# A hybrid encoder step: nine projections as Strassen groups behind the recurrence, with a slot table for all engines

## The chip, the cores and the metric

The kernel runs on one core of a Trainium2 chip. The metric is the device time of one execution in microseconds, lower is better; profiled executions give a span from the first to the last instruction.

## What is computed

One layer of a streaming encoder over 2112 tokens: 2048 of a new stream (16 tiles of 128) and 64 of a running one (the sample, tile 17). From the reference:

```python
xn = rms_norm(x, norm_gain)
u = xn @ w_in                                   # 1024 -> 8 x 1024 columns
xa, za, q, k, v, zb, ga, gb = split_in(u)
xc = conv_b + sum(xpad[:, j:j + T] * conv_w[j] for j in range(CONV_W))
h, h_last = rglru(xc, h0, is_first, ...)        # gates from two block-diagonal products, then a scan
ya = h * jax.nn.silu(za)
q = rms_norm(q.reshape(B, T, H_B, 2, DK), q_norm_gain)
k = rms_norm(k.reshape(B, T, H_B, 2, DK), k_norm_gain)
o = diff_attn(q, k, v, ...)                     # 8 heads, chunk-causal; the sample sees 4096 cached keys
yb = (rms_norm(o, subln_gain) * (1.0 - lam_init)) * jax.nn.silu(zb)
m = jax.nn.sigmoid(ga) * (ya @ w_proj_a) + jax.nn.sigmoid(gb) * (yb @ w_proj_b)
y = x + m @ w_out
```

All of it is float32. Outputs are y, the keys, the values, the last convolution rows and the last recurrence state.

## The kernel before

Every projection is a float32 product made of three passes of the rounded type float32r: an operand is cut into a high part (a rounded copy) and a low part (a subtraction), and `mm3` (L68 to L71) multiplies high by high, high by low and low by high into the same PSUM bank. TensorE runs in the order in which the program issues its work (`manual_schedule`); the other engines are ordered by the compiler's scheduler. The kernel has four stages.

The first (L120 to L347) loads x tile by tile, normalizes it (`norm_x`), transposes it (`turn_x`) and keeps the high and low parts of all of normalized x, channels on partitions, in SBUF (`xh`, `xl`) until the end of the second stage. Values, queries and keys come in twelve blocks of 256 columns: for each token tile `mm_tok` makes 24 matmuls of 256 columns into `acca`, with x as the stationary operand. Queries and keys are normalized per head (`norm_qk`: square, reduction, root, Newton step, scaling) and transposed (`turn_qk`).

The second (L349 to L496) runs over eight channel blocks n. For each, `mm_grp` makes five products (convolution input xa, its gate za, zb, ga, gb) of 128 channels with x as the moving operand, in five token groups of 512, 512, 384, 384 and 320 columns, 24 matmuls per group, into five rotating banks `accb`. `hawk` does the convolution, `gates` the two small gate products one matmul group later, `scan_half` the recurrence of half the tokens; their tiles R, IX, SZ and A have one buffer each. `gated` writes the three gates to DRAM, channel-major.

The third is attention (L498 to L1022), interleaved by a model written in the kernel. Where a head ends, `finish` scales the outputs, and `part` transposes them, multiplies them by the gate zb out of PSUM and writes yb.

The fourth (L1024 to L1086) does the three output projections with weights stationary and activations moving, six groups of 352 tokens, 24 matmuls each per 128 output columns; `load_w3` and `load_g` cut weights and activations on ScalarE, VectorE and GpSimd, and the result is written transposed. Loads and stores go through SP's queue, but for a few on GpSimd's.

The lines around which the change turns are these:

```python
for t in range(0, NT, 2):                       # first stage, per block of 256 columns
    mm_tok(acc[:, j, :], t + j, ws)
for n in range(KT):                             # second stage
    wxa, wza = load_w1(5 * n), load_w1(5 * n + 1)
    hawk(n, wxa, wza)
    gated(load_w1(5 * n + 2), zb_d, n, True)
    gated(load_w1(5 * n + 3), ga_d, n, False)
    gated(load_w1(5 * n + 4), gb_d, n, False)
```

## Time and profile before

| what | value |
|---|---|
| median of 3 runs | 3072.23 us (3063.8 to 3074.84) |
| the profiled execution's span | 3068.5 us |
| first stage (values, queries, keys) | 0 to 663 us |
| second stage (recurrence and gates) | 663 to 1631 us |
| third stage (attention) | 1631 to 2494 us |
| change of stage | 2494 to 2506 us |
| fourth stage (projections) | 2506 to 3065 us |

PE is TensorE's matmuls, PEld its weight loads, DVE VectorE, ACT ScalarE, POOL GpSimd, SPq the queue that issues DMAs. `L57` is line 57 of the kernel, and `out<-in` names the tile that is written and those that are read. In groups the number after the comma is the mean length of one instruction in ns, and what stands after the second bar is the engine's idle time before it. Matmuls are pipelined, so their durations overlap; the distance of their starts is what one costs.

### The profile page before, as it was taken

What the parts mean: (1) busy time and instruction counts of PE and PEld (TensorE: products, weight loads), DVE (VectorE), ACT (ScalarE), POOL (GpSimd) and SP (SyncE); (2) the same over time, 40 slices, a digit from 0 to 9 for tenths busy, and PEclk for the clock granted to TensorE, in tenths of its full rate; (3) what the DMA queues carried; (4) which work ended last, traced back from release to release, by engine and by line L of the source; (5) the groups of instructions that cost most, each with busy time, mean ns of one, the idle gap of its engine ahead of it and who ended that gap; (6) DMA issues with size and microseconds to landing.
All of it is one profiled execution on the core that took longest, in us unless ns stands there. A gap on an engine that the chain in (4) does not pass through costs nothing.

```text
span 3068.5 us, 50185 instructions
## 1 busy us (share of the span) xinstructions
PE 2982.8 (97%) x19448; PEld 2787.9 (91%) x19448; DVE 1322.6 (43%) x3439; ACT 1135.1 (37%) x2179; POOL 1065.5 (35%) x1011
## 2 busy tenths in 40 slices
PE   7999999999999999999998999999999989999999
PEld 7999999999999998999896888888888889999999
DVE  7015454413314224133135667767776761232311
ACT  5112222213224223223134766676676651110100
POOL 1113233222212222122114666666666652222220
PEclk9999999999999999999999999999999999999999
DMA  5223333322121121121117344444543343433322
GB/s 173 81 83 115 125 124 129 120 83 72 39 75 58 43 83 50 45 77 42 64 47 212 107 143 128 127 138 135 147 115 123 94 155 110 122 118 90 94 94 91
DMA packets 208350, 312.37 MB, mean 102 GB/s; under 512 B 33760, under 2 KB 132944, under 8 KB 208112
## 3 DMA queue, kind: packets, MB, share of 16 engines
...
q14 instruction: 84, 0.69, 0.1%
...
## 4 chain that ended last, share of the span: by engine, by line
PE 84%; DVE 7%; ACT 3%; issue 2%; DMA 2%; POOL 1%; SPq 0%; POOLq 0%; ACTq 0%; DVEq 0%
PE accb L71 8%; PE accb L70 8%; PE accb L69 8%; PE acca L69 6%; PE acca L70 6%; PE acca L71 6%; PE acc L71 6%; PE acc L69 6%; PE acc L70 6%; PE accv L640 6%; PE pk L574 3%; PE pk L575 3%; PE ptt L632 3%; PE accv L763 2%; PE pk L695 1%
## 5 line engine op out<-in xcount | busy, mean ns | idle before, releaser
L71 PE MATMUL accb<-xh,wl 128*128 128x512 f32 (+2 forms) x1600 | 562.5, 352 | 0.0
L69 PE MATMUL accb<-xh,wh 128*128 128x512 f32 (+2 forms) x1600 | 562.3, 351 | 0.0
L70 PE MATMUL accb<-xl,wh 128*128 128x512 f32 (+2 forms) x1600 | 562.2, 351 | 0.0
L69 PE MATMUL acca<-wh,xh 128*128 128x256 f32 (+1 forms) x1632 | 469.1, 287 | 0.0
L70 PE MATMUL acca<-wl,xh 128*128 128x256 f32 (+1 forms) x1632 | 461.7, 283 | 2.1 <-DVE wl L131 1.6
L71 PE MATMUL acca<-wh,xl 128*128 128x256 f32 (+1 forms) x1632 | 461.3, 283 | 0.0
L71 PE MATMUL acc<-gh,wl 128*128 128x352 f32 x1152 | 373.6, 324 | 0.0
L69 PE MATMUL acc<-gh,wh 128*128 128x352 f32 x1152 | 373.1, 324 | 0.0
L70 PE MATMUL acc<-gl,wh 128*128 128x352 f32 x1152 | 370.8, 322 | 0.0
L69 PEld LDWEIGHTS accb<-xh,wh 128*128 128x128 f32 x1600 | 300.4, 188 | 25.6
L70 PEld LDWEIGHTS accb<-xl,wh 128*128 128x128 f32 x1600 | 300.3, 188 | 25.5
L71 PEld LDWEIGHTS accb<-xh,wl 128*128 128x128 f32 x1600 | 300.3, 188 | 25.3
L69 PEld LDWEIGHTS acca<-wh,xh 128*128 128x128 f32 (+1 forms) x1632 | 307.7, 189 | 5.4 <-ACT vst L341 3.8
L70 PEld LDWEIGHTS acca<-wl,xh 128*128 128x128 f32 (+1 forms) x1632 | 307.8, 189 | 2.8 <-DVE wl L131 1.8
L71 PEld LDWEIGHTS acca<-wh,xl 128*128 128x128 f32 (+1 forms) x1632 | 307.5, 188 | 0.0
L640 PE MATMUL accv<-v,tw 128*128 128x128 f32 x2176 | 295.3, 278 | 6.3 <-ACT o L652 6.2
L574 PE MATMUL pk<-k,Q 128*128 128x512 f32 (+2 forms) x640 | 266.3, 417 | 29.6 <-DVE mp L595 19.9
L56 POOL TENSOR_SCALAR wh<-raw 128x512 fp32r<-128x512 f32 x125 | 81.7, 654 | 607.9 <-PE accb L70 364.6
L587 DVE TENSOR_SCALAR_CACHE_REDUCE S<-pk,far 128x1024 f32<-128x1024 f32 x224 | 225.8, 1014 | 141.4 <-PE pk L575 131.5
L640 PEld LDWEIGHTS accv<-v,tw 128*128 128x128 f32 x2176 | 270.7, 194 | 10.9 <-ACT o L652 8.3
L605 ACT ACTIVATE S<-S,nm 128x1920 f32<-128x1920 f32 (+7 forms) x128 | 209.0, 1633 | 74.8 <-DVE nm L604 73.3
L575 PE MATMUL pk<-k,Q 128*128 128x512 f32 (+2 forms) x640 | 232.8, 369 | 1.0 <-DMA Q<-ql_d 1.0
...
## 6 DMA issues: line engine op xcount, KB each, us to landing
...
```

Source lines behind the costliest of these rows:

```text
L56: nc.gpsimd.tensor_scalar(hi, src, 1.0, 1.0, op0=ALU.mult, op1=ALU.mult)
L69: nc.tensor.matmul(out, shi, mhi, start=start, stop=False)
L70: nc.tensor.matmul(out, shi, mlo, start=False, stop=False)
L71: nc.tensor.matmul(out, slo, mhi, start=False, stop=stop)
L574: nc.tensor.matmul(pk[:, o], Q[0][:, m, qs], kk, start=True, stop=False)
L575: nc.tensor.matmul(pk[:, o], Q[1][:, m, qs], kk, start=False, stop=True)
L587: nc.vector.tensor_scalar(s[:, k0 : k0 + f], pk[:, :f], far[:, h : h + 1], None, op0=ALU.add, op1=ALU.max, accum_out=mp[:, cx["j"] : cx["j ...
L605: nc.scalar.activation(s[:, :n], s[:, :n], AF.Exp, bias=nm, accum_out=sc[m])
L632: nc.tensor.transpose(ptt[:, j, :], ss[r][:, kt * P : (kt + 1) * P], ident)
L640: nc.tensor.matmul(acc[:, r, :], tw[:, j, :], hd[kt // 8][1][:, kt % 8, :], start=kt == r == 0, stop=kt == 2 * p + 1)
L695: nc.tensor.matmul(pk[:, us], Q, kc[:, us], start=True, stop=True)
L763: nc.tensor.matmul(acc, tw[:, j, :], vc[:, (j8 % 2) * 4 + j, :], start=j8 == 0 and j == 0, stop=False)
```

## The change

The recurrence comes first and alone: per channel block only xa and za are multiplied, with three banks instead of five (three more are for the transposes of x, which now happen inside the first block). Normalized x is put together again on GpSimd (`keep_x`, inside blocks two to four) and written to DRAM.

The nine other projections (values; queries and keys of four heads, twice; zb; ga; gb; the two branch projections; the output projection) become nine groups of 1024 columns. A group takes token tiles in pairs (i and i + 8), cuts x, weights and result into quarters and makes seven products of quarters instead of eight (Strassen's scheme in Winograd's form), each 12 matmuls of 512 columns, with x stationary. The sums of x quarters are made for each pair (`plan_x`), those of weights for each group (`plan_w`), on VectorE and GpSimd. The sample tile has its own form, five slots of 8 matmuls. Time is counted in slots, one for each product: every step of every engine is entered for a slot, and `tick` issues the steps of a slot behind its product, so that TensorE, VectorE, ScalarE and GpSimd all run in the order of the program. Activations and gates are now token-major in DRAM, the gate zb multiplies attention's output before the transpose, and between the second and the third projection the merged activations are transposed on TensorE.

```diff
+class Stage:
+    def __init__(self, nc, tc, c, name, ident):
+        self.nc, self.ident = nc, ident
+        kw = dict(reuse_waits=RW)
+        E = mybir.EngineType
+        c.enter_context(tc.manual_schedule(engines={E.PE, E.DVE, E.Activation, E.Pool}))
+        self.xo = c.enter_context(tc.tile_pool(name="xo" + name, bufs=20, **kw))
+        self.wq = c.enter_context(tc.tile_pool(name="wq" + name, bufs=17, **kw))
+        self.sb = c.enter_context(tc.tile_pool(name="sb" + name, bufs=14, **kw))
+        self.wk = c.enter_context(tc.tile_pool(name="wk" + name, bufs=3, **kw))
+        self.pm = c.enter_context(tc.tile_pool(name="pm" + name, bufs=5, space=PSUM, **kw))
+        self.pt = c.enter_context(tc.tile_pool(name="pt" + name, bufs=3, space=PSUM, **kw))
+        self.now = -99
+        self.tasks = {}
+
+    def at(self, s, fn):
...
+    def plan_w(self, src, ws, b):
+        nc, q, at = self.nc, {}, self.at
+
+        def load(nm, i):
+            q[nm] = self.wtile()
+            for k in range(0, 4, 2):
+                nc.sync.dma_start(q[nm][:, k : k + 2, :], src[i, :, k : k + 2, :])
+
+        def sub(dst, x, y, over=None):
+            q[dst] = q[over] if over else self.wtile()
+            for i in range(2):
+                s = slice(2 * i, 2 * i + 2)
+                nc.vector.tensor_tensor(q[dst][:, s, :], q[x][:, s, :], q[y][:, s, :], op=ALU.subtract)
+
+        def cut(nm):
+            raw = q[nm]
+            hi, lo = self.wtile(F32R), self.wtile(F32R)
+            for i in range(2):
+                s = slice(2 * i, 2 * i + 2)
+                nc.scalar.copy(hi[:, s, :], raw[:, s, :])
+                eng = nc.vector if i == 0 else nc.gpsimd
+                eng.tensor_tensor(lo[:, s, :], raw[:, s, :], hi.bitcast(F32)[:, s, :], op=ALU.subtract)
+            ws[nm] = hi, lo
+
+        at(b - 16, lambda: (load("B11", 0), load("B12", 1)))
+        at(b - 13, lambda: sub("T1", "B12", "B11"))
+        at(b - 10, lambda: load("B22", 3))
+        at(b - 9, lambda: (load("B21", 2), cut("B11")))
+        at(b - 7, lambda: sub("T2", "B22", "T1"))
+        at(b - 6, lambda: cut("T2"))
+        at(b - 5, lambda: sub("T3", "B22", "B12", "B12"))
+        at(b - 4, lambda: sub("T4", "B21", "T2", "T2"))
+        for i, nm in enumerate(("T3", "T1", "B21", "T4", "B22")):
+            at(b - 3 + i, lambda nm=nm: cut(nm))
+
...
+        u, v = item, item + 8
+        at(b - 9, lambda: (load("A21", v, 0), load("A22", v, 1)))
+        at(b - 8, lambda: (load("A11", u, 0), load("A12", u, 1)))
+        at(b - 6, lambda: add(V, "S1", "A21", "A22", ALU.add))
+        at(b - 5, lambda: (add(V, "S2", "S1", "A11", ALU.subtract), add(G, "S3", "A11", "A21", ALU.subtract, "A21")))
+        at(b - 4, lambda: hi("A11"))
+        at(b - 3, lambda: (lo("A11", G), hi("S2")))
+        at(b - 2, lambda: (lo("S2", V), add(G, "S4", "A12", "S2", ALU.subtract), hi("S3")))
+        at(b - 1, lambda: (lo("S3", G), hi("S1")))
+        at(b, lambda: (lo("S1", G), hi("A12")))
+        at(b + 1, lambda: (lo("A12", V), hi("A22"), lo("A22", G)))
+        at(b + 2, lambda: hi("S4"))
+        at(b + 3, lambda: lo("S4", G))
+
+    def product(self, out, a, b, start, stop, more=False):
+        for kt in range(4):
+            mm3(self.nc, out, a[0][:, kt, :], a[1][:, kt, :], b[0][:, kt, :], b[1][:, kt, :],
+                start and kt == 0, stop and kt == 3, more)
+
+    def pair(self, item, x, w, done):
+        nc = self.nc
+        bank = lambda: self.pm.tile([P, 512], F32, name="acc")
+        V = nc.vector
+        b1 = bank()
+        self.product(b1, x["A11"], w["B11"], True, True)
+        u2 = self.small()
+        nc.scalar.copy(u2, b1)
+        self.tick()
+        b2 = bank()
+        self.product(b2, x["S2"], w["T2"], True, True)
+        V.tensor_tensor(u2, u2, b2, op=ALU.add)
+        self.tick()
+        b3 = bank()
+        self.product(b3, x["S3"], w["T3"], True, True)
+        c22 = self.small()
+        V.tensor_tensor(c22, u2, b3, op=ALU.add)
+        self.tick()
+        b4 = bank()
+        self.product(b4, x["S1"], w["T1"], True, True)
+        V.tensor_tensor(c22, c22, b4, op=ALU.add)
+        done(item + 8, 1, c22)
+        self.tick()
+        self.product(b1, x["A12"], w["B21"], False, True, True)
+        c11 = self.small()
+        nc.scalar.copy(c11, b1)
+        done(item, 0, c11)
+        self.tick()
+        self.product(b3, x["A22"], w["T4"], False, True, True)
+        c21 = self.small()
+        V.tensor_tensor(c21, u2, b3, op=ALU.add)
+        done(item + 8, 0, c21)
+        self.tick()
+        self.product(b4, x["S4"], w["B22"], False, True, True)
+        V.tensor_tensor(u2, u2, b4, op=ALU.add)
+        done(item, 1, u2)
+        self.tick()
...
+        bank = lambda: self.pm.tile([P, 512], F32, name="acc")
+        b2 = bank()
+        product(b2, x["A0"], w["B11"], True, False)
+        self.tick()
+        b1 = bank()
+        product(b1, x["A0"], w["B11"], True, False)
+        self.tick()
+        product(b2, x["A0"], w["T1"], False, False)
+        self.tick()
+        product(b1, x["A1"], w["B21"], False, True)
+        out(0, b1)
+        self.tick()
+        product(b2, x["A1"], w["B22"], False, True)
+        out(1, b2)
+        self.tick()
+
+
+    def run(self, groups):
+        plan, b = [], 0
+        for g, (wsrc, xsrc, out) in enumerate(groups):
+            ws = {}
+            self.plan_w(wsrc, ws, b)
+            for it in ITEMS:
+                xs = {}
+                self.plan_x(xsrc, it, xs, b)
+                plan.append((it, xs, ws, out, b))
+                b += 5 if it == "s" else 7
+        self.now = -20
+        while self.now < 0:
+            self.tick() if self.now in self.tasks else self.skip()
+        for it, xs, ws, out, b in plan:
+            assert self.now == b
+            done = out(it, b)
+            if it == "s":
+                self.sample(xs, ws, done)
+            else:
+                self.pair(it, xs, ws, done)
+        while self.tasks:
+            self.tick() if self.now in self.tasks else self.skip()
+
+    def skip(self):
...
+        pm = c1.enter_context(tc.tile_pool(name="pmb", bufs=3, space=PSUM))
+        pg = c1.enter_context(tc.tile_pool(name="pgb", bufs=2, space=PSUM))
...
+        def keep_x(t, half):
+            g, o, tn = tokslice(t)
+            ks = slice(half * 4, half * 4 + 4)
+            raw = wr.tile([P, 4, P], F32, name="raw")
+            nc.gpsimd.tensor_tensor(
+                raw[:, :, :tn], xh[g].bitcast(F32)[:, ks, o : o + tn], xl[g].bitcast(F32)[:, ks, o : o + tn], op=ALU.add
+            )
+            nc.sync.dma_start(xn_d[t, :, ks, :tn], raw[:, :, :tn])
...
+        for n in range(1, KT):
+            hawk(n, load_w1(2 * n), load_w1(2 * n + 1), next_keep)
+        while pend:
+            _, fn, args = pend.pop(0)
+            fn(*args)
...
+        S.run([
+            (I["wg"][0], xn_d, out_v),
+            (I["wg"][1], xn_d, out_qk(0)),
+            (I["wg"][3], xn_d, out_gate(zb_d, True)),
+            (I["wg"][2], xn_d, out_qk(4)),
+            (I["wg"][4], xn_d, out_gate(ga_d, False)),
+            (I["wg"][5], xn_d, out_gate(gb_d, False)),
+        ])
...
+            def weigh(b, nb):
+                tn = TOK[b][1]
+                zt = wk.tile([P, 4, P], F32, name="zt")
+                nc.sync.dma_start(
+                    zt[:tn, :nb, :], zb_d[b : b + nb, :tn, h * P : (h + 1) * P].rearrange("b p c -> p b c")
+                )
+                nc.vector.tensor_tensor(o[:tn, b : b + nb, :], o[:tn, b : b + nb, :], zt[:tn, :nb, :], op=ALU.mult)
...
+                nc.scalar.mul(yt[:, :nb, :tn], pb[:, :nb, :tn], gs)
...
+                at(S.now + 1, lambda: nc.gpsimd.tensor_tensor(c[:tn], c[:tn], gt.pop((t, half))[:tn], op=ALU.mult))
+                at(S.now + 2, lambda: nc.vector.tensor_tensor(c[:tn], c[:tn], mt.pop((t, half))[:tn], op=ALU.add))
...
+        S.run([
+            (I["wg"][6], ya_d, out_a),
+            (I["wg"][7], yb_d, out_b),
+            (I["wg"][8], mt_d, out_y),
+        ])
```

## Rows read from the trace of the kernel before

**Rows 1.** Page, busy time of the span: engine, us, share, instructions.

```profile
PE 2982.8 (97%) x19448; PEld 2787.9 (91%) x19448; DVE 1322.6 (43%) x3439; ACT 1135.1 (37%) x2179; POOL 1065.5 (35%) x1011
```

**Rows 2.** Busy time by stretch: stretch, length, each engine, granted clock, DMA share, GB/s.

```profile
0.00:12.14 12.14, 0.00 (x0) 0.03 (x1) 2.40 (x10) 2.98 (x6) 1.41 (x7) 1.00 0.69 240
12.14:80.00 67.86, 61.23 (x484) 59.27 (x485) 56.70 (x132) 41.98 (x91) 9.85 (x10) 0.97 0.48 156
...
12.14:663.00 650.86, 644.23 (x5319) 634.98 (x5320) 273.69 (x740) 169.67 (x416) 171.26 (x241) 1.00 0.31 112
663.00:1630.70 967.70, 961.84 (x5042) 876.71 (x5042) 291.37 (x475) 287.85 (x405) 241.59 (x270) 1.00 0.19 62
905.00:1026.00 121.00, 120.36 (x633) 109.77 (x632) 36.44 (x59) 35.71 (x50) 30.36 (x33) 1.00 0.17 59
1630.70:2494.00 863.30, 815.73 (x5624) 715.80 (x5622) 612.59 (x1981) 595.71 (x1254) 520.75 (x412) 0.98 0.44 129
2494.00:2506.00 12.00, 1.77 (x12) 1.50 (x13) 10.31 (x19) 5.23 (x10) 8.03 (x9) 0.64 0.76 237
2506.00:3065.00 559.00, 559.00 (x3457) 558.93 (x3456) 131.76 (x214) 73.63 (x91) 122.47 (x74) 1.00 0.36 110
```

**Rows 3.** Timeline of TensorE, first and last matmul of steady runs: start, us, operation.

```profile
20.77 1.03 PE L186 MATMUL ptx<-ident,big 128*128 128x128 f32 x8
...
561.09 0.28 PE L71 MATMUL acca<-wh,xl 128*128 128x256 f32 x1
...
564.09 0.28 PE L69 MATMUL acca<-wh,xh 128*128 128x256 f32 x1
...
722.23 0.40 PE L69 MATMUL accb<-xh,wh 128*128 128x512 f32 x1
...
727.70 0.33 PE L69 MATMUL accb<-xh,wh 128*128 128x384 f32 x1
```

**Rows 4.** Groups by line and shape: busy us, mean ns; L1042 by line: minimum, median, maximum ns.

```profile
L447 DVE TENSOR_TENSOR IX<-sz,xc 128x512 f32<-128x512 f32 x2 | 1.4, 688 | 2.7 <-ACT sz L446 2.7
...
L1042 DVE TENSOR_TENSOR wl<-raw,wh x24: 1214/1225/2735, 2496.7 to 2872.9; 128x1024 fp32r<-128x1024 f32 x24
...
L207 DVE TENSOR_REDUCE va<-sqa 128x8 f32<-128x512 f32 x62 | 42.5, 686 | 254.7 <-ACT sqa L205 254.7
...
L64 DVE SCALAR_TENSOR_TENSOR ya<-tmpa,ya 128x8 f32<-128x8 f32 x61 | 34.4, 564 | 2.1
L246 DVE SCALAR_TENSOR_TENSOR big<-ptx,gq,big 128x256 fp32r<-128x256 f32 x61 | 29.0, 475 | 0.0
...
L57 POOL TENSOR_TENSOR wl<-raw,wh 128x512 fp32r<-128x512 f32 x125 | 162.3, 1299 | 9.7
...
L1058 POOL TENSOR_TENSOR gl<-rg,gh 128x704 fp32r<-128x704 f32 x48 | 83.1, 1741 | 239.1 <-ACT gh L1057 238.8
```

**Rows 5.** VectorE beside GpSimd: two timelines, and two lines with minimum, median, maximum ns.

```profile
L428 DVE SCALAR_TENSOR_TENSOR xc<-xa,chan,xc x120: 544/749/1519, 672.0 to 1562.0; 128x512 f32<-128x512 f32 x48, 128x384 f32<-128x384 f32 x48, 128x324 f32<-128x324 f32 x24
...
712.11 1.52 DVE L428 SCALAR_TENSOR_TENSOR xc<-xa,chan,xc 128x324 f32<-128x324 f32 x1
...
711.97 1.30 POOL L57 TENSOR_TENSOR wl<-raw,wh 128x512 fp32r<-128x512 f32 x1
...
2499.19 1.66 POOL L1058 TENSOR_TENSOR gl<-rg,gh 128x704 fp32r<-128x704 f32 x1 [2.97 <-ACT gh L1057]
2499.20 1.67 DVE L62 SCALAR_TENSOR_TENSOR e<-yo 128x2 f32<-128x2 f32 x1
...
L1077 DVE TENSOR_TENSOR M<-acc,gt x48: 510/525/529, 2515.2 to 2694.1; 128x352 f32<-128x352 f32 x48
```

**Rows 6.** Timelines of ScalarE and VectorE, from one half of a recurrence block to the next.

```profile
691.86 0.48 ACT L402 COPY xa<-accb 128x384 f32<-128x384 f32 x1 [3.59 <-PE accb L71]
...
708.17 1.21 DVE L477 TENSOR_TENSOR SZ<-SZ,R 128x1024 f32<-128x1024 f32 x1
...
713.55 1.00 DVE L417 TENSOR_TENSOR SZ<-sz,accb 128x384 f32<-128x384 f32 x2
```

946 lines of the change are left out of this document (511 added, 435 removed).

## The prediction

> **What bounds the kernel now.** Read the busy table first: TensorE is busy 97% of the span [rows 1]. That word is cheap, since a waiting pipeline can look busy, so the stretches come next [rows 2]. In the value/query/key stretch, in the gate/recurrence stretch and in the projection stretch at the end TensorE has no gap worth naming, while VectorE, ScalarE and GpSimd are busy for a fifth to two fifths. Only attention (815.7 of 863.3 us) and the 12 us between attention and the projections show TensorE idle. Last comes the distance between the starts of matmuls, which is what one really costs (the durations in rows overlap): 24 of 512 columns take 5.47 us, 0.228 each; 25 of 256 columns take 3.00 us, 0.120 each [rows 3]. So each projection stretch costs its matmul count times that distance, and two things can make it shorter: fewer matmuls, or wider ones. The profiled execution spans 3068.5 us; the median of the runs is 3072.2. I add 3.7 us to a sum made in this execution.
>
> **The change, part by part. 1. Products.** Nine products of 1024 columns leave their old forms. Before: 4896 matmuls of 256 columns (values, queries, keys) x 0.120 = 587.5 us. Gates: one pass of the channel loop takes 121.0 us [rows 2] for five column blocks and 30 small recurrence products (12,696 columns at 0.228 per 512 = 5.7 us), so a block is 23.06 us and the 24 gate blocks 553.5 us. Output projections: the whole stretch, 559.0 us. Together 1700 us. After: seven half-size products instead of eight, each 4 slices x 3 passes = 12 matmuls of 512 columns. A pair of token tiles is 84 x 0.228 = 19.14 us; a group is 8 pairs plus 40 matmuls for the sample tile (9.12 us) = 162.3 us; nine groups 1460 us. New on TensorE are 136 transposes of the merged activations, 0.109 us each ((1.03 - 0.27)/7 in [rows 3]) = 14.8 us. The other transposes are as many as before. Saved on TensorE: 225 us. This is the sure part, because the same matmul form (128x128 stationary, 512 moving) stands in the trace.
>
> **2. The recurrence first.** Per channel block TensorE now has 2 x 23.06 + 5.7 = 51.8 us; VectorE keeps 36.4 us less five gate multiplications (some 2.9 us) = 33.5 us, so it fits. Not so the first block, which now also carries the normalization of x. There VectorE did 59.1 us for 17 tiles up to 80 us [rows 2]: 3.4 us per tile without the weights, some 3.65 with the split multiplication: 62 us. With constants (5), fast weights (1.4) and the 20 of 33.5 us that lie ahead of the last column group, started at 8 us (by 12.14 it had done 2.4), this makes 96 us; the last two products add 7: 103 us, where TensorE alone would need 79. Blocks two and three also write the normalized x out again: 15 GpSimd additions each (1.30 us [rows 4]). I take 55 us each (bounds 52, all hidden, and 63, the sum of GpSimd's 38 us and VectorE's 25 us with two SBUF inputs, one after the other), 53 for the fourth and 52 for the rest. Stage: 103 + 110 + 53 + 208 = 474 us (450 to 520).
>
> **3. Who feeds TensorE in the groups.** This is the dangerous part. Before, weights and activations were split once and stayed; now every pair needs 4 VectorE and 7 GpSimd operations of 128x512 to make its sums and low parts, and every group needs 15 VectorE and 7 GpSimd halves of 128x1024 for its weights. Prices [rows 4]: VectorE 0.69 (512) and 1.23 (1024); GpSimd 1.30 (512) and, by the step from 512 to 704 (0.44 us), 2.48 (1024). GpSimd in a plain group: 8 x 9.1 + 17.4 = 90 of 162 us. In the first two projection groups four products of gate and result per pair are added (5.2 us): 134 of 162 and of 177. VectorE in the two query/key groups, per pair: 17 operations of 0.69 (4 for x, 5 out of PSUM, 4 reductions, 4 scalings) = 11.7, two low parts of queries 1.5, two chains of root and Newton steps 2.7: 15.9; weights 18.4/8 = 2.3: 18.2 us against 19.14 + 1.7 = 20.9 us on TensorE.
>
> These two engines don't run free of each other. The trace shows it three times [rows 5]: a VectorE operation of 128x324 with two SBUF inputs that takes 0.54 alone takes 1.52 when it starts inside a GpSimd subtract, and ends 0.36 after it; a Newton step of two columns takes 1.67 beside a subtract of 1.66; the product that reads PSUM never took over 0.53. The wait is a little shorter than the whole: 1.16 + 0.54 would be 1.70, measured 1.52. So an operation with two SBUF inputs waits out the other engine's, about half a GpSimd operation each time. In a query/key pair 14 VectorE operations are of that kind and GpSimd is busy two thirds: 14 x 2/3 x 0.6 = 5.6 us; 18.2 + 5.6 = 23.8 against 20.9, 2.9 us per pair, 24 per group, with the weight boundary 28 (0 to 45). The Trainium skill, in "SBUF — State Buffer", section "Who interferes with whom", states this as an exclusive lock: a VectorE instruction with two SBUF inputs and a GpSimd instruction that reads SBUF block each other for a whole instruction. By that rule taken whole the groups would go as in rival B below; the trace agrees with the lock, short of the 0.18 us just worked out.
>
> Where groups meet, the weights' 35.8 us of VectorE and GpSimd work fall into 13 slots before the group and 6 slots of it (8 x 2.73 + 5 x 1.82 + 6 x 2.73 = 47 us), beside 24 us of x work (6 left of the last pair, 1 for the sample, 17 for the next two pairs): 59 us with whole durations, less where they overlap. I take 4 us where the neighbours are light (twice), 6 after the gate group with SiLU, 28 with each query/key group, 10 at each of the two boundaries of the projections: 90 us in all (0 to 180).
>
> **4. Seams.** Recurrence to groups: the weight space is the old x space and comes free only as the last block uses it; 12 us (2 to 25). Groups to attention: 5 (0 to 12), the first keys wait for x tiles. Attention: weighting by the gate moves ahead of the transpose, VectorE's product stays one, ScalarE gets 41 copies in 863 us; I take 863 (-5 to +10), since the transposes there waited only a little on VectorE. Attention to projections: 12 us now, with DMA at 237 GB/s [rows 2]; the first group needs 4 MB of weights and 1 MB of x, 21 us at that rate, some of it ahead: 22 (12 to 35). Queue: all of these loads sit on SP, and a store that waits for a result holds the loads behind it; the table issues loads 8 to 16 slots ahead (22 us and more), which covers a landing of 3 to 5 us. End: a DMA and two additions more: 8 instead of 3.5.
>
> Sum: 474 + 12 + (6 x 162.3 + 272 x 0.109 + 2 = 1005) + 70 + 5 + 863 + 22 + (3 x 162.3 + 14.8 = 501.6) + 20 + 8 = 2980; plus 3.7: **2984 us**, 88 less than the median.
>
> **Rivals. A, TensorE stays fed.** The slot leads of 3 to 5 slots (8 to 14 us) swallow the waits: no 90, the first seam 4, the second 0, the third 12, the recurrence 450: 2847 us. For it: GpSimd has 90 of 162 us in five groups. Against: query/key and the two projection groups.
> **B, the shared path sets the pace.** GpSimd and two-input VectorE work add up with whole durations: first projection group 132 + 41 = 173 against 162 us (+11), second, with 4 more additions on VectorE per pair, 197 against 177 (+20), 12 us at each of seven boundaries (84), query/key 30 each: 175 instead of 90 us, 3069 us (3040 to 3095). For it: [rows 5]. Against: the 0.18 us of overlap per wait, over some 100 waits in a group. The page named above, taken whole, would give this.
> **C, slower: a convoy.** All four engines run in emission order. If in the four crowded groups each of the 61 slots waits for one more GpSimd subtract, 244 x 1.30 = 317 us come in place of 76: 3225 us. It takes the whole gain from 0.67 us per slot ((88 + 76)/244). Against: results are two slots old when their bank is written again.
> **D, three banks.** The recurrence has 3 PSUM banks for its products where it had 5, and one buffer for the gated product: from the evacuation at 691.86 to the end of the product that frees it 17.5 us pass, and the bank of the next half goes free after 713.55 [rows 6]. If TensorE waits there, 5.5 and 4 us per block, 65 in all: 3048 us. Against: with two banks held the third still turns over.
>
> **How the numbers follow.** Chances: forecast 0.54 (2900 to 3040), A 0.15, B 0.15, D 0.06, C 0.10. The range reaches down to the upper half of A and up to B's middle: 2855 to 3070; outside are half of A, some of B, and C. This kernel's measurement can tell about 0.5% from no change, so faster is below 3057 and slower above 3087. Faster: 0.53 + 0.15 + 0.06 + 0.04 = 0.78; within: 0.01 + 0.07 + 0.02 = 0.10; slower: 0.10 + 0.02 = 0.12.
>
> **What would show it.** Right: groups of about 162 us in plain stretches, query/key groups near 205, x work on VectorE lengthened from 0.69 towards 1.5 while GpSimd subtracts, TensorE's idle time ending on VectorE or GpSimd operations of the weights near group starts, the recurrence over at about 474 us. Wrong: TensorE idle in every slot (C), idle ended by the gated product's buffer (D), a pair above 19.5 us without any wait (the matmul price), or attention longer by more than 10 us.

## The result and the profile after

The changed kernel takes 3253.1 us in the median, the kernel before 3073.1 us in the same series: a ratio of 1.059 (95% interval 1.058 to 1.061). The forecast was 2984 us with a range of 2855 to 3070. Both the sign and the range were missed. The profiled execution spans 3249.5 us.

The busy table of after, to set beside [rows 1] (engine, us, share, instructions):

```profile
PE 2866.6 (88%) x14808; PEld 2396.7 (74%) x14808; DVE 2111.9 (65%) x3884; ACT 1564.5 (48%) x2871; POOL 1826.5 (56%) x1311
```

TensorE has fewer instructions, as meant, but it is busy 88% of the span instead of 97%; VectorE and GpSimd have risen from 43% and 35% to 65% and 56%.

Busy time by stretch in after, the counterpart of [rows 2] (stretch, length, PE, PEld, DVE, ACT, POOL, granted clock, DMA share, GB/s):

```profile
0.00:127.00 127.00, 81.52 (x448) 72.64 (x449) 91.70 (x252) 83.01 (x166) 23.63 (x32) 0.87 0.30 101
127.00:526.00 399.00, 375.15 (x1898) 335.86 (x1896) 261.63 (x382) 187.25 (x240) 182.71 (x165) 0.97 0.19 61
526.00:559.00 33.00, 0.27 (x2) 0.01 (x1) 16.49 (x16) 11.62 (x12) 2.80 (x2) 0.55 0.49 176
559.00:1709.00 1150.00, 1050.59 (x4560) 840.89 (x4560) 760.39 (x900) 484.49 (x850) 662.09 (x423) 0.96 0.42 132
1709.00:1729.00 20.00, 0.03 (x1) 0.06 (x1) 1.50 (x3) 2.70 (x4) 7.02 (x18) 0.54 1.02 263
1729.00:2656.00 927.00, 837.35 (x5632) 727.02 (x5632) 620.87 (x1998) 613.34 (x1296) 531.25 (x410) 0.96 0.42 118
2656.00:2675.00 19.00, 0.17 (x1) 0.00 (x0) 8.95 (x7) 4.91 (x7) 2.47 (x2) 0.50 0.94 336
2675.00:3241.00 566.00, 521.34 (x2272) 420.26 (x2272) 347.76 (x325) 176.62 (x299) 414.52 (x262) 0.95 0.49 164
3241.00:3249.50 8.50, 0.16 (x1) 0.00 (x0) 2.57 (x4) 0.58 (x1) 0.00 (x0) 0.63 0.26 63
```

The reader can lay this beside the forecast's sum, stretch by stretch (boundaries by first and last matmul):

| stretch | forecast, us | measured, us | missed by |
|---|---|---|---|
| recurrence | 474 | 526 | +52 |
| to the groups | 12 | 33 | +21 |
| six groups | 1075 | 1150 | +75 |
| to attention | 5 | 20 | +15 |
| attention | 863 | 927 | +64 |
| to the projections | 22 | 19 | -3 |
| three groups | 522 | 566 | +44 |
| end | 8 | 8 | 0 |

The misses add up to 268 us, and no single one explains the result. That is why the experiments go stage by stage.

What was right is seen in a plain pair (first line; 86 matmuls and no idle time) beside a query/key pair (second line):

```profile
1050.00:1069.00 19.00, 19.00 (x86) 15.74 (x85) 9.66 (x13) 7.07 (x15) 10.13 (x8) 1.00 0.31 111
822.80:845.60 22.80, 21.14 (x102) 17.20 (x101) 18.95 (x31) 10.87 (x21) 12.01 (x9) 1.00 0.54 162
```

The plain pair takes 19.0 us, forecast 19.14. Six of the nine groups run so once they are under way (in the value group two pairs also hold 16 small matmuls for the position strips and take 22.1 and 24.5 us); the second projection group takes 21.0 us, with four times four transposes more per pair. The query/key pair has 1.66 us without a matmul. The largest losses lie at the starts. The first pairs of the nine groups take 40.2, 33.6, 25.2, 35.7, 26.7, 33.5, 40.2, 35.5 and 26.7 us. That is 123 us more than their matmuls at 0.228 us. For 83 of them TensorE stands idle (waits over 0.1 us); behind such waits matmuls also start further apart, at a lower clock (0.77 granted over the first of these pairs, 559.03 to 599.20).

### The profile page after: what moved, and what is told of

It reads as the page before. It is cut to its first block, busy times and chain, and to the rows that moved or that the text cites. A ratio compares the mean times of both kernels' runs of the same rounds, so it can differ in the third digit from the quotient of the medians.

```text
span 3249.5 us, 43984 instructions
## 1 busy us (share of the span) xinstructions
PE 2866.6 (88%) x14808; PEld 2396.7 (74%) x14808; DVE 2111.9 (65%) x3884; ACT 1564.5 (48%) x2871; POOL 1826.5 (56%) x1311
## 3 DMA queue, kind: packets, MB, share of 16 engines
q10 hardware_dynamic: 2240, 1.15, 0.1%
## 5 line engine op out<-in xcount | busy, mean ns | idle before, releaser
L70 PE MATMUL acc<-w,xq 128*128 128x512 f32 x2016 | 802.9, 398 | 80.3 <-POOL xq L169 64.7
L68 PE MATMUL acc<-w,xq 128*128 128x512 f32 x2016 | 810.6, 402 | 54.5 <-ACT xq L166 52.0
L69 PE MATMUL acc<-w,xq 128*128 128x512 f32 x2016 | 799.4, 397 | 0.0
L169 POOL TENSOR_TENSOR xq<-xq 128x512 fp32r<-128x512 f32 x360 | 532.4, 1491 | 348.9 <-ACT xq L166 239.7
L70 PEld LDWEIGHTS acc<-w,xq 128*128 128x128 f32 x2016 | 386.5, 192 | 176.7 <-POOL xq L169 73.3
L68 PEld LDWEIGHTS acc<-w,xq 128*128 128x128 f32 x2016 | 387.2, 192 | 139.7 <-ACT xq L166 53.4
L69 PEld LDWEIGHTS acc<-w,xq 128*128 128x128 f32 x2016 | 386.9, 192 | 78.6
L166 ACT CAST xq<-xq 128x512 fp32r<-128x512 f32 x504 | 298.9, 619 | 38.3 <-PE acc L69 19.3
L879 PE MATMUL pk<-k,Q 128*128 128x512 f32 (+2 forms) x640 | 264.7, 415 | 49.0 <-DMA Q<-qh_d 20.4
L162 POOL TENSOR_TENSOR xq<-xq 128x512 f32<-128x512 f32 x144 | 210.2, 1460 | 90.8 <-DVE xq L162 76.0
L136 POOL TENSOR_TENSOR w<-w,w 128x1024 fp32r<-128x1024 f32 x63 | 183.0, 2904 | 129.9 <-ACT w L134 110.0
L68 PE MATMUL accb<-xh,wh 128*128 128x384 f32 (+3 forms) x656 | 235.2, 359 | 0.2 <-ACT xh L461 0.2
L69 PE MATMUL accb<-xl,wh 128*128 128x384 f32 (+3 forms) x656 | 233.1, 355 | 1.0 <-DVE v L439 0.8
L918 POOL TENSOR_TENSOR S<-S,S 128x2048 f32<-128x2048 f32 (+3 forms) x64 | 231.5, 3618 | 4.3
L70 PE MATMUL accb<-xh,wl 128*128 128x384 f32 (+3 forms) x656 | 232.6, 355 | 0.0
```

What stands on the lines that cost most here:

```text
L68: nc.tensor.matmul(out, shi, mhi, start=start, stop=False, **kw)
L69: nc.tensor.matmul(out, shi, mlo, start=False, stop=False, **kw)
L70: nc.tensor.matmul(out, slo, mhi, start=False, stop=stop, **kw)
L162: eng.tensor_tensor(q[dst], q[x], q[y], op=op)
L166: nc.scalar.copy(xs[nm][0], q[nm])
L169: eng.tensor_tensor(xs[nm][1], q[nm], xs[nm][0].bitcast(F32), op=ALU.subtract)
```

## The experiments

Times are medians; the changed kernel is 3253.1 us. "Head" is the mean distance from one head's first sample score to the next, over six heads: 106.8 us before, 114.4 after.

### Who feeds TensorE where groups meet

The timelines of VectorE and GpSimd in after, at the start of the last gate group, and the matmul that waits there (start, us, engine, line, operation, shape, count):

```profile
1536.39 5.60 DVE L136 TENSOR_TENSOR w<-w,w 128x1024 fp32r<-128x1024 f32 x2
1541.91 1.77 DVE L169 TENSOR_TENSOR xq<-xq 128x512 fp32r<-128x512 f32 x1
1543.61 5.64 DVE L136 TENSOR_TENSOR w<-w,w 128x1024 fp32r<-128x1024 f32 x2
...
1535.34 2.25 POOL L169 TENSOR_TENSOR xq<-xq 128x512 fp32r<-128x512 f32 x1
1537.56 3.35 POOL L136 TENSOR_TENSOR w<-w,w 128x1024 fp32r<-128x1024 f32 x1
1540.87 2.27 POOL L162 TENSOR_TENSOR xq<-xq 128x512 f32<-128x512 f32 x1
1543.09 2.86 POOL L136 TENSOR_TENSOR w<-w,w 128x1024 fp32r<-128x1024 f32 x1
...
1537.65 0.80 PE L70 MATMUL acc<-w,xq 128*128 128x512 f32 x1 [4.70 <-POOL xq L169]
```

and line 136 as a whole (minimum, median, maximum ns):

```profile
L136 POOL TENSOR_TENSOR w<-w,w x63: 2337/2831/3431, 549.4 to 3084.7; 128x1024 fp32r<-128x1024 f32 x63
L136 DVE TENSOR_TENSOR w<-w,w x63: 1209/2286/3448, 553.9 to 3079.2; 128x1024 fp32r<-128x1024 f32 x63
```

Both engines lie there without a gap, and both are stretched. A half that takes VectorE 1.21 us at best takes 2.29 in the median, and GpSimd's own operations grow as well (1.30 to 2.25; 2.34 to 3.35). In the forecast only VectorE waited. TensorE waits 4.70 us for the low part of x that GpSimd ends behind such a wait.

**e3_weights_vector**

```diff
-                eng = nc.vector if i == 0 else nc.gpsimd
-                eng.tensor_tensor(lo[:, s, :], raw[:, s, :], ...
+                nc.vector.tensor_tensor(lo[:, s, :], raw[:, s, :], ...
```

> The second half of each weight's low part is subtracted by VectorE too, no longer by GpSimd: seven halves of 128x1024 a group, 2.16 us each on GpSimd when nothing hinders it, 1.21 us on VectorE. Theory 'one path': where groups meet, two-input work on VectorE and GpSimd adds up with whole durations in both directions (3.37 us = 1.21 + 2.16 on either engine), 59 us of it into 47; VectorE alone needs 8.5 us for what took GpSimd 15: the first pairs of the groups (33.6, 25.2, 35.7, 26.7, 33.5, 40.2, 35.5, 26.7 us) become 4 to 7 us shorter each, the kernel 3210 us (3195 to 3230). Rival 'two engines': they run beside each other and only the later one counts; then VectorE, which has 18 of the 33 us, gets 8.5 us more per boundary, the first pairs become longer and the kernel 3253 to 3310 us.

Measured: 3209.6 us. VectorE got 63 operations more and the kernel became 43 us shorter. (GpSimd's half takes 2.34 us at best in the trace above, not the 2.16 of the expectation.) The first pairs of the second to eighth groups went to 28.7, 25.0, 31.1, 23.8, 28.1, 35.8 and 31.5; only the ninth grew (30.3). "Two engines" is refuted. But a GpSimd that is simply the slower engine would have given a gain too; e3 alone doesn't tell that from a shared path.

**e10_x_vector**

```diff
-        V, G = nc.vector, nc.gpsimd
+        V, G = nc.vector, nc.vector if light else nc.gpsimd
...
+        # light: every group but the two of queries and keys
```

> Beside the weights' halves (as in the third run) all sums and low parts of x are made by VectorE in the seven groups that are not query/key, so GpSimd does no two-input work there but the products with the projection gates. Theory 'one path': the two engines never ran beside each other on such work, so VectorE alone, at 0.69 us for what takes GpSimd 1.30, shortens the crowded starts further: first pairs of 28.7, 25.0, 31.1, 23.8, 28.1, 35.8, 31.5 and 30.3 us in the third run become 3 us shorter at six of them, the kernel 3190 us (3180 to 3203) against 3209.6 of the third run. Rival 'VectorE is full': 27 us of weights, 18 of x and 9 of evacuations out of PSUM don't fit into the 47 us of slots of a group's start, and the sums now stand in one row: first pairs stay or get longer, the kernel 3210 us or more.

This stands on top of e3. Measured: 3159.1 us, 94 less than the changed kernel and more than expected. The groups by line in this kernel, and below them the same lines in after (busy us, mean ns, idle before and its releaser):

```profile
L168 DVE TENSOR_TENSOR xq<-xq 128x512 fp32r<-128x512 f32 x256 | 180.5, 730 | 0.0
L135 DVE TENSOR_TENSOR w<-w,w 128x1024 fp32r<-128x1024 f32 x82 | 103.7, 1308 | 11.4 <-ACT w L134 11.4
```

```profile
L169 DVE TENSOR_TENSOR xq<-xq 128x512 fp32r<-128x512 f32 x96 | 99.7, 1038 | 0.0
L136 DVE TENSOR_TENSOR w<-w,w 128x1024 fp32r<-128x1024 f32 x40 | 93.7, 2357 | 2.4 <-ACT w L134 2.4
```

In the six groups VectorE makes twice as many halves of weights in almost the same busy time, 103.7 us for 82 against 93.7 for 40. Over the same stretch its busy time rises from 760 to 804 us, while GpSimd's falls from 662 to 235. VectorE took over 42 halves of weights and 224 operations on x, 205 us at 1.21 and 0.69 us each, and is busy only 44 us longer. The work taken from GpSimd was, in effect, already being waited for on VectorE. That is what tells the shared path from a slow GpSimd.

Not all of the 94 us come from the feeding. By stretches, 75 us are gained in the nine groups, and 17 in the seam before attention (20.4 to 2.9 us), where GpSimd asks for the first keys at 1647.2 us, ahead of the last product, and not behind it. The first pairs are still 73 us longer than their matmuls. In the longest two of them VectorE alone is busy for 29 to 30 of 31 us, so there one engine's work is the limit.

**e4_turn_late**

```diff
-                        at(S.now + 5 + i, lambda m=m: turn_qk(h0, *m))
+                        at(S.now + 7 + i, lambda m=m: turn_qk(h0, *m))
```

> Query/key groups only: the transposes of the scaled queries and keys are emitted two slots later (7 and 8 slots behind their result, not 5 and 6). Theory 'latency': TensorE waits 1.82 us per pair because VectorE's scaling stands at the end of a chain (square, sum, root, Newton, two scalings) that is longer than its slots, while VectorE is busy 19.0 of 22.8 us; two slots more cover it: pairs go from 22.8 to 21.0 us, and the sample item with what follows it (20.2 + 7.0 us) becomes some 5 us shorter: 2 x (7 x 1.8 + 5) = 35 us, the kernel 3218 us (3208 to 3235). Rival 'rate': VectorE held up by GpSimd is the pace itself, slack moves the wait and nothing else: pairs stay above 22.3 us and the kernel within 8 us of 3253.

Measured: 3225.9 us. The pairs did go from 22.8 to 21.0 to 21.4 us, so in the pairs the wait was latency. But the gain was mostly handed on: the query/key groups became 21 and 23 us shorter, and the first pairs of the groups behind them went from 25.2 and 26.7 to 42.7 us. The stalls of all groups together fell only from 208 to 195 us. The other half of the gain came from elsewhere. The first keys for attention were asked for ahead of the last product, not behind it, and the 20 us in front of attention shrank to less than one. What this kernel does to the buffers at that place was not followed further.

### Attention

Counted score product by score product against the kernel before, after loses its time in one place of each head: at the sample's scores and the 12 us behind them. Timeline of VectorE there, after:

```profile
2099.73 1.28 DVE L1004 TENSOR_SCALAR_CACHE_REDUCE SA<-pk,far 128x1024 f32<-128x1024 f32 x1
...
2104.17 1.28 DVE L1004 TENSOR_SCALAR_CACHE_REDUCE SA<-pk,far 128x1024 f32<-128x1024 f32 x1
...
2109.47 0.85 DVE L1107 TENSOR_TENSOR o<-o,zt 128x512 f32<-128x512 f32 x1 [4.01 <-POOL o L1127]
2111.29 0.85 DVE L1107 TENSOR_TENSOR o<-o,zt 128x512 f32<-128x512 f32 x1 [0.96 <-POOL o L1127]
2112.06 1.27 DVE L1004 TENSOR_SCALAR_CACHE_REDUCE SB<-pk,far 128x1024 f32<-128x1024 f32 x1
...
2115.16 0.69 DVE L1107 TENSOR_TENSOR o<-o,zt 128x512 f32<-128x512 f32 x1 [1.21 <-DMA zt<-zb_d]
2116.72 0.28 DVE L1107 TENSOR_TENSOR o<-o,zt 64x128 f32<-64x128 f32 x1 [0.86 <-DMA zt<-zb_d]
2116.93 1.14 DVE L1004 TENSOR_SCALAR_CACHE_REDUCE SB<-pk,far 128x896 f32<-128x896 f32 x1
```

The four L1004 operations empty the banks of the sample's scores. Between them stand the five products with the gate (four are shown), which wait in brackets for GpSimd's scaling and for the gate to land. The fourth evacuation starts 17.2 us after the first. In the kernel before it is 6.4 us, and the product with the gate, there taken out of PSUM into `yt`, comes behind:

```profile
1990.12 1.26 DVE L699 TENSOR_SCALAR_CACHE_REDUCE SA<-pk,far 128x1024 f32<-128x1024 f32 x1
...
1996.52 1.15 DVE L699 TENSOR_SCALAR_CACHE_REDUCE SB<-pk,far 128x896 f32<-128x896 f32 x1 [1.75 <-PE pk L695]
...
1997.81 0.74 DVE L806 SCALAR_TENSOR_TENSOR yt<-ptt,gs,zt 128x512 f32<-128x512 f32 x1
```

**e1_weigh_late**

```diff
-                weigh(b, nb)
+                late = h < NH - 1
+                extras.append([pe[0] + (6.5 if late else 0.0) + 1.5 * j, 0.0, lambda b=b, nb=nb: fetch(b, nb)])
+                extras.append([pe[0] + (9.3 if late else 1.0) + 1.5 * j, 0.0, lambda b=b, nb=nb: weigh(b, nb)])
```

> Attention only: the load of the gate and VectorE's product with it are put 6.5 and 9.3 us behind the end of a head in the order of emission, ahead of the transposes as in the changed kernel. In the changed kernel the product stands in VectorE's order right behind the root, waits there for GpSimd's seventeen scalings (0.43 us each, waits of up to 4.0 us), and the evacuations of the score banks queue behind it: 114.4 us per head against 105.5 before. Theory 'order': per head about 106 us again, the attention stretch from 927 to 870 us (865 to 885), the kernel 3196 us (3185 to 3212). Rival 'pieces': the gate and the result now move in pieces of 512 bytes, and ScalarE waits for the store of yt (30.7 us in 9 waits): then the stretch stays above 905 us and the kernel above 3230 us.

Measured: 3248.4 us, heads 114.8. The theory's price was missed altogether, because the products still ran between the evacuations.

**e5_gate_gpsimd** and **e6_yt_vector**

```diff
-                nc.vector.tensor_tensor(o[...], o[...], zt[...], op=ALU.mult)
+                nc.gpsimd.tensor_tensor(o[...], o[...], zt[...], op=ALU.mult)   # e5
...
-                nc.scalar.mul(yt[...], pb[...], gs)
+                nc.vector.tensor_scalar(yt[...], pb[...], gs, None, op0=ALU.mult)   # e6
```

> Attention only: the product of the head outputs with the gate (41 operations, four token tiles each) goes from VectorE to GpSimd, right behind GpSimd's scalings. What the first run of attention left: the compiler orders VectorE by itself, and moving the emission put the five products of a head no later; they stand among the evacuations of the sample's scores and take 0.85, 0.85, 0.91, 2.20 and 2.59 us (0.69 alone) with two waits of 0.9 us between them. Theory 'product': these 9 us on VectorE, where TensorE waits for each evacuation, are the nine us that a head got longer: without them attention goes from 927 to 885 us (870 to 900), the kernel to 3211 us (3195 to 3228); GpSimd has 5.6 us more per head and stands at 60%. Rival 'ScalarE': the five evacuations of the turned outputs, now on ScalarE behind two exponentials of 2 us, are the cause (TensorE waits 3.45 us for one in each head): then attention stays above 912 us and the kernel above 3238 us.

> Attention only: the turned outputs are scaled out of PSUM by VectorE (as one operation with one input from PSUM, as in the kernel before), no longer by ScalarE; the product with the gate stays on VectorE ahead of the transposes. Theory 'product' (VectorE's two-input products among the sample's evacuations): attention stays above 912 us, or gets longer by up to 10 us, for VectorE has five more operations of 0.75 us per head. Rival 'ScalarE': the waits of 3.45 us per head for these evacuations go, with the ScalarE waits for the stores of yt (30.7 us), and attention goes to 895 us (880 to 905), the kernel to 3221 us.

Measured: e5 3284.1 us, heads 119.4; e6 3241.5 us, heads 112.8. In e5 the cure is worse: the chain to the transposes gets longer, TensorE comes to them in its fixed order and waits 38 us in 23 waits for GpSimd's products. So e5 doesn't test the theory, it replaces one wait by another. In e6 ScalarE's share turns out to be under 2 us per head.

**e9_weigh_far**: as e1, with 19, 22 and 26 us (the transposes).

> Attention only: the first try put the product with the gate 9.3 us behind the end of a head, and the trace shows that this is still among the sample's scores (20 us of work at the start of each head). Here the load of the gate, VectorE's product and the transposes are emitted 19, 22 and 26 us behind the end of a head. Counted score product by score product, the changed kernel loses its time against the kernel before at one place of each head, the sample's scores and the 12 us behind them. Theory 'VectorE's queue': there VectorE waits for GpSimd's scalings (4.0 and 1.0 us) and for the gate to land (1.2 and 0.9 us) while the evacuations of the sample's scores, for which TensorE waits, stand behind (the four evacuations are spread over 17.2 us, 6.4 before). Behind the sample's scores the product costs nothing: heads of 114.4 us become 106 (105 to 108), the kernel 3196 us (3187 to 3208). Rival 'more work': the extra operations as such (ScalarE's evacuations, the stores in pieces of 512 bytes, the two-input products) cost 9 us per head wherever they stand: heads stay at 112 us or more, the kernel above 3236 us.

Measured: 3230.4 us, heads 111.2; the attention stretch is 910 us instead of 927. The same waits of 4.02, 0.97 and 1.15 us stand in VectorE's timeline between the evacuations. Only TensorE keeps the order of emission in this stage; where VectorE's operations go is the compiler's decision, and it takes the product as soon as its operands are there.

**e13_weigh_behind** and **e14_no_product**

```diff
+                late[0] = wk.tile([P, 1], F32, name="late")      # e13, behind the sample's maximum
+                nc.vector.tensor_scalar(late[0], nm, 0.0, 1.0, op0=ALU.mult, op1=ALU.add)
...
-                nc.vector.tensor_tensor(o[...], o[...], zt[...], op=ALU.mult)   # left out in e14
+                nc.vector.scalar_tensor_tensor(o[...], o[...], late[0][:tn], zt[...],
+                                               op0=ALU.mult, op1=ALU.mult)      # e13
```

> Attention only: as in the ninth run, and VectorE's product with the gate also multiplies by a column of ones that VectorE makes from the sample's maximum, so it can't run before the last evacuation of the sample's scores. The ninth run (heads of 111 us) showed why this is wanted: wherever the product was emitted, VectorE ran it between the sample's evacuations as soon as GpSimd's scalings let it (waits of 4.0, 1.0 and 1.2 us there), for in attention only TensorE keeps the order of emission. Theory 'VectorE's queue': with the evacuations (17.2 us apart in the changed kernel, 6.4 before) running through first, heads are 107 us (105.5 to 108.5), the kernel 3200 us (3188 to 3212). Rival 'more work': the operations themselves cost it wherever they stand; heads stay at 110.5 us or more and the kernel above 3224 us.

> Attention only, a price: VectorE's product with the gate is left out (the gate is still loaded; the head outputs go on unweighted), all else as in the changed kernel. Theory 'VectorE's queue': what a head lost (114.4 against 105.5 us) comes from these five products alone: 106.5 us (105.5 to 108.5), the kernel 3197 us (3185 to 3212). Rival 'more work': ScalarE's evacuations of the turned outputs (behind exponentials of 2 us, TensorE waits up to 3.1 us for one) and the stores in short pieces are the larger part: heads stay at 110.5 us or more, the kernel above 3224 us.

e13 keeps e9's later load and transposes. Measured: e13 3180.9 us, heads 105.3; e14 3195.9 us, heads 106.6. Attention takes 866 us in e13 and 870 in e14, against 863 in the kernel before. The timeline of VectorE in e13 at the same place:

```profile
2077.25 1.28 DVE L1006 TENSOR_SCALAR_CACHE_REDUCE SA<-pk,far 128x1024 f32<-128x1024 f32 x1
...
2081.69 1.28 DVE L1006 TENSOR_SCALAR_CACHE_REDUCE SA<-pk,far 128x1024 f32<-128x1024 f32 x1
...
2082.89 1.28 DVE L1006 TENSOR_SCALAR_CACHE_REDUCE SB<-pk,far 128x1024 f32<-128x1024 f32 x1
...
2085.05 1.15 DVE L1006 TENSOR_SCALAR_CACHE_REDUCE SB<-pk,far 128x896 f32<-128x896 f32 x1 [0.87 <-PE pk L1002]
...
2087.16 0.76 DVE L1120 SCALAR_TENSOR_TENSOR o<-o,late,zt 128x512 f32<-128x512 f32 x1
```

The evacuations run through in 7.8 us and the product follows. Leaving the product out gains no more than putting it behind, so nearly all of the 64 us is a matter of place, not of added work: 17 us go with e9's later load and transposes, and another 45 with the dependency that holds the product behind the evacuations.

### The recurrence and the first block

GpSimd in block two of after (timeline; L469 is the addition that writes x out, L54 and L55 split the channel rows), and below it the two matmuls that wait for the split:

```profile
142.27 5.54 POOL L469 TENSOR_TENSOR raw<-xh,xl 128x512 f32<-128x512 f32 x2
147.78 0.61 POOL L54 TENSOR_SCALAR ch<-xc 128x512 fp32r<-128x512 f32 x1
148.48 2.11 POOL L55 TENSOR_TENSOR cl<-xc,ch 128x512 fp32r<-128x512 f32 x1
150.55 2.68 POOL L469 TENSOR_TENSOR raw<-xh,xl 128x512 f32<-128x512 f32 x2
...
148.45 0.79 PE L68 MATMUL pr<-ch,ghi 128*128 128x512 f32 x1 [3.96 <-POOL ch L54]
...
150.64 0.80 PE L69 MATMUL pr<-cl,ghi 128*128 128x512 f32 x1 [1.40 <-POOL cl L55]
```

**e2_keep_spread**

```diff
             if kept:
-                keep_x(*kept.pop(0))
+            calls[0] += 1
+            if kept and calls[0] % 3 == 1:
+                keep_x(*kept.pop(0))
```

> Recurrence only: GpSimd's 34 additions that write the normalized x out are emitted at every third call in blocks two to eight, not at every call in blocks two to four. Theory 'GpSimd's queue': the additions (1.37 us each, fifteen in blocks two and three) stand ahead of the split of the channel rows, TensorE waits 9 us in each block for it and runs at a granted clock of 0.90; spread out, five of them per block are hidden: blocks two and three go from 65.8 and 67.2 to 53 or 54 us, the others stay under 54, the stage ends near 500 us instead of 525 (495 to 510), the kernel 3229 us (3222 to 3240). Rival 'three banks' (the forecast's rival D): the missing two PSUM banks and the single buffer of the gated product hold these blocks; then they stay above 62 us and the kernel within 6 us of 3253.

Measured: 3266.8 us, 14 more. Blocks two to eight take 60.4, 61.7, 61.8, 58.4, 60.5, 58.3 and 54.4 us: neither theory foresaw that thin spreading would hurt everywhere. In its trace the additions stand in a row at the start of each block, ahead of the split. TensorE there (timeline):

```profile
389.98 0.40 PE L68 MATMUL pr<-ch,ghi 128*128 128x512 f32 x1
392.73 0.51 PE L69 MATMUL pr<-cl,ghi 128*128 128x512 f32 x1 [2.35 <-POOL cl L55]
...
394.09 0.63 PE L68 MATMUL accb<-xh,wh 128*128 128x512 f32 x1
394.51 0.63 PE L69 MATMUL accb<-xl,wh 128*128 128x512 f32 x1
```

The wait of 2.35 us isn't the whole price: from 394.09 on seven matmuls start 0.43 us apart, at the lower level of 1.2 GHz (the granted clock is 0.50 from 394.1 to 397.0), and not 0.228 apart as at 2.4 GHz. That is 1.4 us more.

**e7_no_add** and **e12_keep_vector**

```diff
-            nc.gpsimd.tensor_tensor(raw[...], xh[...], xl[...], op=ALU.add)
+            nc.sync.dma_start(xn_d[t, :, ks, :tn], xh[g].bitcast(F32)[:, ks, o : o + tn])   # e7: no addition
...
+            nc.vector.tensor_tensor(raw[...], xh[...], xl[...], op=ALU.add)                 # e12: e2 on VectorE
```

> Recurrence only: GpSimd's 34 additions are left out; the stores of the normalized x go straight from its high part (so the low part is missing from what the groups read). After the second run (additions called less often: every block became 5 to 8 us longer, and the trace shows that the compiler puts them in a row at the start of each block whatever the place of the call), theory 'GpSimd beside the channel split': an addition costs TensorE 0.8 to 1.6 us wherever it stands, partly as a wait for the split, partly as matmuls at the lower clock behind that wait. Without them blocks two, three and four go from 65.8, 67.2 and 54.5 to 53, 53 and 52.5 us, the stage from 525 to 496 us (493 to 503), the kernel to 3224 us (3216 to 3233). Rival 'stores and banks': the 34 stores and loads beside them or the three PSUM banks hold these blocks: then they stay above 60 us and the kernel above 3240 us.

> Recurrence only: the second run once more (additions called at every third place), with the additions on VectorE instead of GpSimd: 0.69 us each, 34 of them. Theory 'GpSimd beside the channel split': what costs TensorE 5 to 8 us in each block of the second run is that GpSimd's additions stand ahead of the split of the channel rows and hold up VectorE's two-input work; on VectorE, which is busy 34 of 52.5 us, they add 3.4 us per block in one engine and nobody waits for the other: blocks go from 60 to 53.5 us (52.5 to 55), the stage ends near 503 us, the kernel 3231 us (3224 to 3240). Rival 'any addition': the chain from convolution to split, which is on VectorE as well, is what has no room; then blocks stay at 57 us or more, the kernel above 3250 us.

Measured: e7 3225.1 us, blocks two to seven 52.5 us each; e12 3232.0 us, those blocks 53.9 to 54.5. Blocks two and three of e7 (first fence) and of e12 (second; stretch, length, busy times, clock):

```profile
128.20:233.20 105.00, 103.72 (x543) 94.01 (x542) 65.56 (x108) 53.16 (x68) 37.94 (x39) 1.00 0.13 42
```

```profile
125.70:234.20 108.50, 104.54 (x542) 93.77 (x540) 71.74 (x117) 52.43 (x67) 43.10 (x40) 1.00 0.20 67
```

Without GpSimd's 34 additions two blocks take 105.0 us with three PSUM banks, TensorE busy 103.7. That refutes rival D. The same additions on VectorE cost some 1.5 us per block.

**e8_no_root_table**

```diff
-            nc.scalar.activation(sq[:tn], v[:tn], AF.Sqrt)
+            nc.scalar.activation(sq[:tn], v[:tn], AF.Square)
```

> First block only: the root in the normalization of x is left out (ScalarE squares in its place, so x is scaled by a wrong number), because ScalarE has to load a table of functions each time it goes between the root and the sigmoids of the gates: 21 loads of 1.28 us, 27 us, in the first 127 us of the changed kernel, against 2 in the first 130 us of the kernel before. Theory 'tables': most of the 24 us by which the first block was missed comes from there; some 10 loads go (13 us), the first block from 104.4 to 92 us (88 to 97), the kernel to 3241 us (3235 to 3247). Rival 'VectorE': VectorE (84 of the first 113 us busy) sets the pace as the forecast had it, and the loads are hidden beside it: the block stays above 100 us, the kernel within 5 us of 3253.

Measured: 3245.8 us; the first block 95.4 instead of 104.4 us, its end at 116.5 instead of 127.1. So "VectorE" is refuted, and "tables" holds for 10.5 of the 24 us, not for most of them; 6 of the 21 loads are left. Three of the nine groups of table loads that ScalarE has in the first 127 us of after (count, busy us, ns):

```profile
L441 ACT ACT_TABLE_LOAD x8 | 10.3, 1283 | 1.2 <-DVE v L439 0.9
L536 ACT ACT_TABLE_LOAD x3 | 3.8, 1283 | 0.1
L577 ACT ACT_TABLE_LOAD x3 | 3.8, 1283 | 0.1
```

L441 is the root of the normalization, L536 and L577 are sigmoids of the gates: 21 loads in all. The Trainium skill, "ScalarE: Activation LUTs", section "What ACT_TABLE_LOAD costs", gives: a load takes about 1283 ns whatever the set; the trace agrees, with 1283 in the mean of every group. The same section adds a drain of about 1380 ns to a switch; here the trace shows none: an operation ends at 84.27 us, the load starts at 84.29, and the next operation at 85.59.

### The seams, and everything together

**e11_first_loads**

```diff
-                nc.sync.dma_start(q[nm][:, k : k + 2, :], src[i, :, k : k + 2, :])
+                self.queue(b).dma_start(q[nm][:, k : k + 2, :], src[i, :, k : k + 2, :])
...
+        return self.nc.gpsimd if b == 0 else self.nc.sync
```

> The loads of weights and activations for the first pair and first group of each of the two group stages go through GpSimd's queue, not SP's. In the changed kernel the first weights are asked for at 541.75 us, behind SP's stores of the last half of the recurrence, which wait for its scan (539.5 us), while TensorE has nothing to do from 526.3 and GpSimd from 525.2. Theory 'queue': the loads start at 527, the first product of the groups at 545 instead of 559 us, the kernel 3238 us (3233 to 3244). Rival 'space': the weights' space is that of the tiles of the last scan, and comes free with them; the first product stays within 4 us of 559, the kernel within 6 of 3253.

Measured: 3245.1 us. The first product of the groups came at 557.7 instead of 559.0 us: "space" was right for this seam. Two of the eight weight loads start at 523.8 us, the other six at 542.3, when the store of the last scan's result has landed; in after all eight start at 541.75. Most of the gain that the profile shows is in the first pair of the projections (35.7 for 40.2 us).

**c1_vector_feeds, c2_and_attention, c3_first_loads_too**: e10, e12 and the pairs' part of e4; then e13 added; then e11 added.

> Three single finds together: weights and, outside query/key groups, activations cut by VectorE alone (tenth run, 94 us less than the changed kernel), the additions of the recurrence on VectorE at every third place (twelfth run, 21 us less), and the transposes of the query/key pairs two slots later, but not those of the sample (in the fourth run pairs went from 22.8 to 21.2 us, while the sample's later transposes gave back 17 us at the start of the next group). Theory 'separate stages': they add up: 3253 - 94 - 21 - 2 x 7 x 1.7 = 3114 us (3100 to 3130). Rival 'given back': VectorE in the query/key groups has the weights too and no slack left, pairs stay above 22.3 us, or the next group's start gets longer by what the pairs gain: 3133 us or more.

> The run before this one and the product behind the sample's evacuations (thirteenth run). If the forecast's misses are these separate causes and no common one (TensorE's clock, memory), the gains add up: 3114 - 53 = 3061 us (3045 to 3078), within 0.5% of the kernel before (3072), while the kernel is still longer than the forecast by the space hand-over at the two ends of the groups, the first block and the crowded group starts. Rival 'common cause': the gains overlap and the kernel stays above 3090 us.

> The run before (all causes found, 3063.6 us) with the first loads of both group stages on GpSimd's queue as in the eleventh run, where that gave 8 us: the first product came only 1.3 us sooner, because six of eight weight loads still waited for the space of the last scan, but the first pair of the output projections went from 40.2 to 35.7 us. Theory 'space': the same here, 3 to 8 us: 3058 us (3054 to 3063). Rival: with VectorE doing the cuts the first pairs (30.5 and 31.6 us) wait for VectorE and no longer for loads; then nothing changes (3061 to 3066 us).

Measured: c1 3130.4 us, c2 3063.6, c3 3066.0. In c1 the query/key pairs are 21.0 to 21.4 us, but the first pairs behind these groups 34.8 instead of 24.2 and 23.5: of the 24 us about five a group are left, nearer to "given back". c2 then gained 67 us and not 53, close to the 72 us of e13 alone. So these gains do add up, and no cause that they share is seen. c2 is 0.2% faster than the kernel before: ratio 0.998, interval 0.997 to 0.999. c3 shows no further gain.

By stretches, c2 (a span of 3062 us) stands 82 us above the forecast's sum: recurrence 506 for 474, the seam behind it 32 for 12, groups 1095 for 1075 and 536 for 522. The seam before attention, attention and the seam behind it (3, 864 and 18) are where the forecast put them, within 4 us.

## Why the prediction was wrong, step by step

**1. Products: right.** Pairs of 19.0 us for 19.14, sample items without a wait 9.3 to 9.4 for 9.12; half of the 72 pairs run at that pace, and TensorE's part of the sum holds. The 225 us are saved, and 406 us are lost elsewhere.

**2. Recurrence: mis-sized, +52.** The first block ended at 127 us, not 103. I priced VectorE alone; ScalarE's table loads (2 in the kernel before in as long a stretch, 21 now) are 10.5 of the 24 us by e8. The cause of the other 13.5 stays open. Blocks two and three took 133 us, not 110 and not the upper bound of 126: I added up the two engines' busy time, and left out that the additions stand ahead of the split on GpSimd and that TensorE runs slower behind each wait. e7 and e12 give the term over all blocks: 30 us on GpSimd (397.6 less 367.7 us for blocks two to eight), 9 on VectorE.

**3. Feeding the groups: the step that failed first.** The working had 59 us of work against 47 us of slots "with whole durations", and then took 4 to 10 us per boundary "less where they overlap", from rows in which a VectorE operation overlapped a GpSimd one by 0.18 us [rows 5]. They hardly overlap: in the rows above both engines wait, for nearly the whole of the other's operation (up to 3.43 and 3.45 us for what takes 2.34 and 1.21 at best; the sum is 3.55). Measured stalls are 208 us where I put 90: 1715 us of groups less 1507 of matmuls and transposes. Of these 123 stand in the nine first pairs and 60 in the other query/key pairs with their samples. Rival B, by whole durations in one path, had 175 and was the right mechanism for the first pairs; in the query/key pairs e4 shows a chain that is longer than its slots. I gave B 0.15 and an "against", the 0.18 us, that weighs nothing. The sum also took each stall at its length, while the first pairs lose 123 us with 83 of waiting. The shared path isn't all of it: with most of GpSimd's share on VectorE (e10), 133 of the 208 us stay, and 124 in c2. The Trainium skill's rule of the lock ("SBUF — State Buffer", "Who interferes with whom") was taken for one side only; the trace agrees with it on both, and e10 decides for it.

**4. Seams: mis-sized, +36 in two of three.** I had named space for both, with 12 and 5 us. At the first I counted on the space of x, free with the last block's products. By e11 six of the eight weight loads wait for the store of the last scan's result, until 16 us behind the last product (526.3 to 542.3), and then 4 MB of weights and the first activations have to land. At the second the first keys wait for space that the last product of the groups still reads, as GpSimd's wait list of after shows (waited for, us, times, longest):

```profile
POOL k L823 <- PE acc L245: 13.0, 1, 13.0
```

Then the loads keep the DMA engines fully busy for 20 us, at 263 GB/s (the stretch from 1709 to 1729).

**5. Attention: mis-sized, +64, bounds -5 to +10.** "VectorE's product stays one" counts the operation and not its place. Ahead of the transposes it follows GpSimd's scaling directly, in the 20 us in which TensorE waits for VectorE's evacuations of the sample's scores (28.8 us in ten waits over the stage); behind them, as in the kernel before, it waited for TensorE. I didn't name what is queued behind it.

**Rivals.** A and D are refuted. C's 3225 us is near the result by accident: in the crowded groups that it spoke of, the steady pairs of the two projection groups take 19.0 and 21.0 us, without a wait, and a query/key pair loses 1.9 us and not seven times 1.30, so there was no convoy. B was right for the starts of the groups and silent on 150 of the 268 us. The forecast's sum had one sure saving, and of its terms the recurrence, two seams and attention stood in the lower half of the bounds that I gave and the feeding in the middle. All five were missed on the same side, and a range to 3070 left no room for that.
